# Memory queries in two token halves, rounding behind the second spatial mix, branch weights requested step by step

## The chip, the core and the metric

The kernel runs on one core of one Trainium2 chip. The metric is the device time of one execution in microseconds (us). The time before is the median of three runs, 2185.58 us (2185.37 to 2185.59). About 0.2% of it, 4.4 us, is what a measurement of this kernel can tell from no change.

## What is computed

One decoder layer over 1024 tokens of width 1024, all in float32: half a SwiGLU block, a mixing block with three branches, half a SwiGLU block. The change is in the mixing block:

```python
h = rmsnorm(x); z = h @ w_in
u, v = gelu(z[u]), gelu(z[v])
v = layernorm(v)                                   # chunks of 128 tokens, 8 groups of 64 channels
mixed = einsum('gts,bcsgd->bctgd', tril(w_s), v) + b_s
y_a = u * mixed                                    # branch a
y_b = mla(...)                                     # branch b, 8 heads, causal
q = rmsnorm(z[q_mem]); kv = rmsnorm(mem) @ w_kv    # 256 memory tokens, 4 heads of 128
k = rmsnorm(kv[:512]); s = q @ k.T * 128**-0.5
y_c = softmax(s) @ kv[512:]                        # branch c
merged = sum_i sigmoid(gate_i) * (y_i @ w_branch_i)
x = x + merged @ w_out
```

## The kernel before

Float32 products are made of three fast products. An operand is split in a rounded high part and a low part (`split`, L135: a cast on ScalarE, ACT, at L136, and a subtraction on VectorE, DVE, at L139), and `mm3` (L157) multiplies high by high (L160), high by low (L161) and low by high (L162). A weight can thus be used in full only when both engines have had their turn with it.

Tokens go in two halves of 512. The stretch in question is `sgu` (L570) and `mem_attention` (L824), about 1100 to 1205 us into the span. In program order it holds:

- `mem_kv` (L774) up to its first yield: the product for the memory keys, and their norm (`head_norm`).
- `split(1)` (L577), which rounds the second half of v, and a one-column Exp that brings in the table for the softmax (L610).
- `mix(0)` (L582): eight groups of three matmuls, each into a PSUM bank and from there to SBUF with a bias by ACT (L591), then for each of four channel blocks a load of u (L594), four transposes (L597), the product with u on DVE (L598), and `split_after` (L141; cast L142, subtraction L143).
- The rest of `mem_kv`: the product for the memory values, the keys turned and split into `kt` (L795, which ends in L152 on ACT and L153 on DVE), the values split into `vv` (L799).
- `mix(1)`: the same for the second token half.
- `mem_queries` (L814): the four heads' queries, high and low part, 8 loads of 128 x 1024 elements (512 KB), ordered behind the last load of u.
- `branches` (L503) of branch a, a generator. `weights` (L510) loads and splits 128 x 1024 weights for a pair of output blocks; a step loads the gate values (L521, 256 KB), does 12 matmuls of one block and one token half (`branch`, L551) and hands the bank to `sink_a` (L1044: L1045 on DVE, a store at L1046). The first three steps are blocks 0, 1, 2 of the first half, then the same of the second half, then each block's two halves. Blocks 0 and 1 use the first and the second 512 columns of the first pair of weights.
- `mem_attention`, which takes turns by a written list (L874): F is a branch step, S the scores of one tile of 128 tokens (12 matmuls of 256 columns, L834; then minimum L838, scaling L839, Exp L843, sum L847, scaling on GpSimd L848), T transposes, V the product with the values. It begins F, F, S, F, S, F, F, T, S.

PSUM gives this stretch four single banks ("bank", for the mix, the transposes and the branch steps) and two double ones ("mm", for the products of `mem_kv` and for the scores). In SBUF there are three raw buffers for unsplit weights, six rows "t" for u and the gates, and 16 "h" buffers.

The written order is not the order on the engines. In this stretch a planner of the framework orders them: when the program is built it runs a model of the machine (L2213), and gives an engine that is free the earliest instruction in program order whose inputs and buffers the model takes to be ready. On the chip each engine then keeps to its list. `after(i, first)` (L414) forces a place: i stands behind first on their common engine, without a semaphore. `self.hold` makes every cast of `split` stand behind an instruction in that way, and as long as it is set, `fetch` (L92) puts its load behind `self.queue`, the last store of the queries of branch b (L498). All DMAs here are issued by SyncE's queue (SP), in the planner's order.

Of the kernel before, what the change touches and what calls it, by code (L numbers as in the profile page):

```python
# [8 lines left out]
F32 = mybir.dt.float32  # L9
# [3 lines left out]
ACT = mybir.ActivationFunctionType  # L13
ALU = mybir.AluOpType
# [4 lines left out]
S = 1024  # L19
DT = D // P  # L20
NT = S // P
F = 2816
FT = F // P
SGW = 512
# [25 lines left out]
class Kernel:  # L50
# [1 line left out]


    def __init__(self, ctx, tc, a, out):
        self.tc, self.nc, self.a, self.out, self.last, self.hold = tc, tc.nc, a, out, None, None
        pool = lambda name, bufs=1, **k: ctx.enter_context(tc.tile_pool(name=name, bufs=bufs, **k))
        self.const = pool("const")
        self.small = pool("small", 4)
        self.hp = pool("hp", 16)
        self.xp = pool("xp", 10)  # L60
        self.wp = pool("wp")
        self.tp = pool("tp")
        self.ps = pool("ps", 1, space=bass.MemoryType.PSUM)
        self.dram = pool("dram", 1, space=bass.MemoryType.DRAM)
# [27 lines left out]
    def fetch(self, src, rooms=()):  # L92

        n, width = src.shape[1:]
        per, rooms = D // width, list(rooms)
        for k0 in range(0, n, per):
            m = min(per, n - k0)
            raw = rooms.pop(0)().rearrange("p a w -> p (a w)") if rooms else self.raw()
            raw = raw[:, :m * width]
            i = self.nc.sync.dma_start(raw, src[:, k0:k0 + m, :].rearrange("p k w -> p (k w)"))  # L100
            if self.hold is not None:
                self.after(i, self.queue)
            yield m, width, raw

# [30 lines left out]
    def split(self, hi, lo, src, eng=None):  # L135
        i = self.nc.scalar.copy(hi, src)  # L136
        if self.hold is not None:
            self.after(i, self.hold)
        return (eng or self.nc.vector).tensor_tensor(lo, src, hi.bitcast(F32), op=ALU.subtract)  # L139

    def split_after(self, hi, lo, src):  # L141
        i = self.nc.scalar.copy(hi, src)  # L142
        self.nc.vector.tensor_tensor(lo, src, hi.bitcast(F32), op=ALU.subtract)  # L143
        return i

    def split_later(self, hi, lo, src):

# [291 lines left out]
    def qkv(self, lat, asides):  # L439
# [3 lines left out]
        half = ROPE // 2  # L443
# [3 lines left out]
        T = 2  # L447
        with tc.tile_pool(name="qkvp", bufs=1) as p, tc.tile_pool(name="q1", bufs=1) as p1:
            for i0 in range(0, NT, 2):
# [45 lines left out]
                    nc.sync.dma_start(d, k[:, t].rearrange("p (g x) d -> p g (x d)", x=2))  # L495
                for t in range(T):
                    d = self.qd[:, :, i0 + t].rearrange("g p e -> p g e")
                    self.queue = nc.sync.dma_start(d, q[:, t].rearrange("p (g x) d -> p g (x d)", x=2))  # L498
                if i0 == T:
                    self.qk_mark = mark  # L500
                next(asides, None)
# [1 line left out]
    def branches(self, br, yt, sink):  # L503

        nc, a, w = self.nc, self.a, {}

        steps = [(dt, hf) for hf in range(2) for dt in range(3)]
        steps += [(dt, hf) for dt in range(3, DT) for hf in range(2)]

        def weights(d):  # L510
            if d not in w:
                x = self.load(a["w_branch"][br, d // 2])
                w[d // 2 * 2], w[d // 2 * 2 + 1] = x[:4], x[4:]

        weights(0)
        yield
        for n, (dt, hf) in enumerate(steps):
            for d, _ in steps[n:n + 2]:
                weights(d)
            sig = self.row()  # L520
            nc.sync.dma_start(sig, self.sig[br * DT + dt][:, hf])  # L521
            b = self.bank()
            self.branch(b, w[dt], yt, hf)
            sink(dt, hf, sig, b)
            yield
# [44 lines left out]
    def sgu(self, rows, p, sink):  # L570
        nc, a, tc = self.nc, self.a, self.tc
        v8 = lambda tag, hf, dt=F32R: (p if hf else self.pv).tile([P, 4, SGW], dt, name=tag)
        if True:
            w = self.parts_of(self.wss, P, self.split_pair)
            vs, yt = {}, []

            def split(hf):  # L577
                vs[hf] = v8("v_hi", hf), v8("v_lo", hf)
                for i, v in enumerate(rows[hf]):
                    self.v_mark = self.split(*(x[:, 2 * i:2 * i + 2] for x in vs[hf]), v)  # L580

            def mix(hf):  # L582
                if not yt:
                    yt.extend(self.split_pair() for _ in range(4))
                m, v = [self.h4().rearrange("p a w -> p (a w)") for _ in range(2)], vs[hf]
                views = [x.rearrange("p (c g d) -> p c g d", g=4, c=4) for x in m]
                for g in range(SGG):
                    b = self.bank()[:, :4 * SGW // SGG].rearrange("p (c d) -> p c d", c=4)
                    cols = slice(g * SGW // SGG, (g + 1) * SGW // SGG)
                    self.mm3(b, w[g], tuple(x[:, :, cols] for x in v), True, True)  # L590
                    nc.scalar.activation(views[g // 4][:, :, g % 4], b, ACT.Identity, bias=self.sg_b[:, g:g + 1])  # L591
                for j in range(4):
                    u = self.row()
                    z = nc.sync.dma_start(u, self.z[ZU + j][:, hf])  # L594
                    b = self.bank()
                    for c in range(4):
                        nc.tensor.transpose(b[:, c * P:(c + 1) * P], views[j // 2][:, c, 2 * j % 4:2 * j % 4 + 2], self.ident)  # L597
                    nc.vector.tensor_tensor(u, u, b, op=ALU.mult)  # L598
                    i = self.split_after(*(t[:, hf * 512:hf * 512 + 512] for t in yt[j]), u)
                return i, z  # L600

            self.hold = self.turned
            split(0)
            self.hold = None
            for v in rows[1]:
                self.layer_norm(v, self.qk_mark)
            kv = self.mem_kv(self.mem_t, self.mem_w)
            next(kv)
            split(1)
            nc.scalar.activation(self.stat("warm", 1), vs[1][0][:, 3, SGW - 1:].bitcast(F32), ACT.Exp, scale=0.0)  # L610
            mark, _ = mix(0)
            kv = next(kv)
            _, z = mix(1)
            rooms = [v8(n, 0).rearrange("p (a b) w -> p a (b w)", a=2) for n in ("v_hi", "v_lo")]
            late = self.mem_queries(1, iter([tuple(x[:, i] for x in rooms) for i in range(2)]), z)
            queries = self.mem_queries(0, iter(lambda: self.split_pair(self.h4), None), z) + late
            branch = self.branches(0, yt, sink)
            self.hold = mark
            next(branch)
            self.hold = None  # L620
            rooms = [v8(n, 1, F32) for n in ("v_hi", "v_lo")]
            rooms = [x.rearrange("p (a h) (b m) -> p a (h b) m", a=2, b=2)[:, k] for x in rooms for k in range(2)]
            return self.mem_attention(queries, rooms, *kv, branch)

    def head_norm(self, x, ps):

# [147 lines left out]
    def mem_kv(self, mt, w):  # L774
# [19 lines left out]
        for hh in range(0, MH, 2):  # L794
            self.to_feature(  # L795
                tuple(t[:, hh:hh + 2].rearrange("p h m -> p (h m)") for t in kt),
                [x[:, t, hh + k] for k in range(2) for t in range(2)], self.mk_g,
            )
        self.split(vv[0], vv[1], ps)  # L799
        yield kt, vv  # L800

# [9 lines left out]
            out += [tuple(t[:, i * 512:i * 512 + 512] for t in ts) for i in range(2)]  # L811
        return out

    def mem_queries(self, pair, rooms, first):  # L814

        out = []
        for o in range(2):
            qs = next(rooms)
            for t, src in zip(qs, self.mq[2 * pair + o]):
                self.after(self.nc.sync.dma_start(t.bitcast(F32), src), first)  # L820
            out.append(qs)
        return out

    def mem_attention(self, qt, rooms, kt, vv, filler):  # L824

        nc = self.nc
        r, nr = self.mq_r, self.mq_nr
# [2 lines left out]
        def scores(i, k):  # L830
            t = 2 * i + k
            sc = self.mm().rearrange("p a (b m) -> p (a b) m", b=2)
            for hh in range(MH):
                self.mm3(  # L834
                    sc[:, hh], tuple(x[:, t * P:(t + 1) * P] for x in qt[hh]), tuple(x[:, hh] for x in kt),
                    True, True)
            mx = self.stat("m_mx", MH)
            nc.vector.tensor_reduce(mx, sc, axis=AXX, op=ALU.min)  # L838
            nc.vector.tensor_tensor(mx, mx, r[:, t], op=ALU.mult)  # L839
# [30 lines left out]

        S, T, V = scores, turn, value
        F = lambda: next(filler, None)
        yt = [self.split_pair(self.h4) for _ in range(MH)]
        for f, *x in (  # L874
                (F,), (F,), (S, 0, 0), (F,), (S, 0, 1), (F,), (F,), (T, 0, 0), (S, 1, 0), (F,), (T, 0, 1), (S, 1, 1),
                (F,), (V, 0), (F,), (T, 1, 0), (S, 2, 0), (F,), (T, 1, 1), (S, 2, 1), (F,), (V, 1), (F,), (T, 2, 0),
                (S, 3, 0), (F,), (T, 2, 1), (S, 3, 1), (F,), (V, 2), (F,), (T, 3, 0), (F,), (T, 3, 1), (F,), (V, 3)):
            f(*x)
# [1338 lines left out]
```

## Time and profile before

| | |
|---|---|
| median of three runs | 2185.58 us |
| the profiled execution | 2181.75 us |
| its span | 2180.0 us |
| TensorE (PE) busy | 2160.0 us, 99% |
| DVE busy | 1574.5 us, 72% |
| ACT busy | 911.4 us, 42% |
| granted TensorE clock | 0.999 |

The profile is one execution. Its times count from the start of the span. Rows of the timeline give the start, the time from start to end, the engine, the line, the operation, what it writes and reads, and how many instructions are merged in the row; in brackets stands how long the engine was idle before, and who ended it. PE is TensorE's matmuls, SPq the issues of DMAs. Rows by windows give each engine's busy time in a stretch, with the granted clock, the busy share of the DMA engines and what they moved. An idle time counts for the whole only if it is on the engine that sets the end.

### The profile page before, as it was taken

The numbers are of one execution on the slowest core, as the hardware profiler recorded it, in microseconds if no ns is written. First come the engines' busy times: TensorE is split into PE (matmuls) and PEld (weight loads), VectorE is DVE, ScalarE is ACT, GpSimd is POOL, SyncE is SP. The second block draws the span as 40 slices with busy tenths as digits, with TensorE's granted clock in tenths as the row PEclk, the third lists the DMA queues.
The fourth block names the chain that finished last, engine by engine and source line by source line (L and its number), as shares of the span: only waits on it lengthen the run. The fifth ranks groups of instructions, "written<-read, shape, count | busy, mean of one in ns | idle before, by whom it ended". The sixth has DMA issues, their size and how long they took to land.

```text
span 2180.0 us, 27531 instructions
## 1 busy us (share of the span) xinstructions
PE 2160.0 (99%) x10154; PEld 1802.9 (83%) x10154; DVE 1574.5 (72%) x2374; ACT 911.4 (42%) x1491; POOL 273.5 (13%) x278
## 2 busy tenths in 40 slices
PE   9999999999999999999999999999999999999999
PEld 5888888888887888888988889988888888888887
DVE  7976666679889656655895679885886666657884
ACT  5433333343445334433554368833432222224332
POOL 2011111100000000000232321140011211210000
PEclk9999999999999999999999999999999999999999
DMA  4264554385433444541685731093043233337443
GB/s 146 92 218 163 185 176 174 137 319 172 130 116 104 147 166 166 209 147 61 231 320 217 266 121 59 30 351 123 34 140 102 93 101 99 114 130 291 169 130 106
DMA packets 128823, 340.98 MB, mean 156 GB/s; under 512 B 15152, under 2 KB 23472, under 8 KB 128688
## 3 DMA queue, kind: packets, MB, share of 16 engines
q1 hardware_dynamic: 128688, 339.22, 44.5%
q8 instruction: 80, 1.31, 0.2%
q14 instruction: 55, 0.45, 0.1%
HBM read 229.33 MB, written 109.84 MB: 156 GB/s over the span
## 4 chain that ended last, share of the span: by engine, by line
PE 91%; DVE 5%; ACT 2%; issue 1%; DMA 1%; POOL 0%; SPq 0%; ACTq 0%; DVEq 0%; POOLq 0%
PE one L160 15%; PE one L161 15%; PE one L162 15%; PE bank L160 12%; PE bank L162 12%; PE bank L161 12%; PE mm L160 2%; PE mm L161 2%; PE mm L162 2%; PE bank L968 1%; PE bank L983 1%; PE bank L984 1%; PE bank L432 1%; DVE wlo L149 1%; DVE wlo L139 0%
## 5 line engine op out<-in xcount | busy, mean ns | idle before, releaser
L148 ACT CAST whi<-x 128x1024 fp32r<-128x1024 f32 (+1 forms) x203 | 193.2, 955 | 419.4 <-PE one L161 141.7
L149 DVE TENSOR_TENSOR wlo<-x,whi 128x1024 fp32r<-128x1024 f32 (+1 forms) x203 | 242.2, 1194 | 57.9 <-ACT whi L148 21.6
L1376 DVE TENSOR_TENSOR t<-t,one 128x512 f32<-128x512 f32 x188 | 129.0, 686 | 194.0 <-PE one L162 193.8
L160 PE MATMUL bank<-h,whi 128*128 128x512 f32 x636 | 247.6, 390 | 0.0
L162 PE MATMUL bank<-h,wlo 128*128 128x512 f32 x636 | 247.5, 389 | 0.0
L161 PE MATMUL bank<-h,whi 128*128 128x512 f32 x636 | 247.5, 389 | 0.0
L160 PE MATMUL one<-h,whi 128*128 128x512 f32 x516 | 202.3, 392 | 0.0
L161 PE MATMUL one<-h,whi 128*128 128x512 f32 x516 | 201.5, 391 | 0.0
L162 PE MATMUL one<-h,wlo 128*128 128x512 f32 x516 | 201.3, 390 | 0.0
L160 PE MATMUL one<-w,whi 128*128 128x512 f32 x432 | 168.6, 390 | 0.0
L162 PE MATMUL one<-w,wlo 128*128 128x512 f32 x432 | 168.1, 389 | 0.0
L161 PE MATMUL one<-w,whi 128*128 128x512 f32 x432 | 168.1, 389 | 0.0
L139 DVE TENSOR_TENSOR wlo<-w,whi 128x1024 fp32r<-128x1024 f32 (+2 forms) x112 | 114.7, 1038 | 70.1 <-ACT whi L136 69.9
L136 ACT CAST whi<-w 128x1024 fp32r<-128x1024 f32 (+2 forms) x112 | 99.0, 901 | 149.8 <-PE bank L161 53.7
L1958 POOL TENSOR_TENSOR raw<-raw 128x512 f32<-128x512 f32 x38 | 56.9, 1498 | 783.6 <-DVE raw L1813 684.8
L162 PEld LDWEIGHTS bank<-h,wlo 128*128 128x128 f32 x636 | 119.4, 188 | 24.9
L161 PEld LDWEIGHTS bank<-h,whi 128*128 128x128 f32 x636 | 119.4, 188 | 24.7
L160 PEld LDWEIGHTS bank<-h,whi 128*128 128x128 f32 x636 | 119.4, 188 | 24.6
L160 PE MATMUL bank<-whi 128*128 128x512 f32 x352 | 136.9, 389 | 0.0
L161 PE MATMUL bank<-wlo,whi 128*128 128x512 f32 x352 | 136.9, 389 | 0.0
L162 PE MATMUL bank<-whi,wlo 128*128 128x512 f32 x352 | 136.9, 389 | 0.0
L162 PEld LDWEIGHTS one<-h,wlo 128*128 128x128 f32 x516 | 97.3, 189 | 20.3
(391 smaller groups left out, 4913.2 us busy)
## 6 DMA issues: line engine op xcount, KB each, us to landing
x<-in_ffn_w_gu_dram SPq DMA_DIRECT2D x78, 512.0 KB, 4.9
w<-tdt SPq DMA_DIRECT2D x40, 512.0 KB, 4.5
gate<-raw SPq DMA_DIRECT2D x33, 512.0 KB, 2.9
tdb<-raw SPq DMA_DIRECT2D x64, 256.0 KB, 2.2
h<-in_ffn_w_down_dram SPq DMA_DIRECT2D x64, 256.0 KB, 6.0
w<-tdb SPq DMA_DIRECT2D x30, 512.0 KB, 4.4
tdt<-w SPq DMA_DIRECT2D x48, 256.0 KB, 2.3
x<-in_w_gate_dram SPq DMA_DIRECT2D x22, 512.0 KB, 7.1
```

Source lines behind the costliest of these rows:

```text
L136: i = self.nc.scalar.copy(hi, src)
L139: return (eng or self.nc.vector).tensor_tensor(lo, src, hi.bitcast(F32), op=ALU.subtract)
L148: self.nc.scalar.copy(hi, src)
L149: return lambda: self.nc.vector.tensor_tensor(lo, src, hi.bitcast(F32), op=ALU.subtract)
L160: i = mmul(out, s[0], m[0], start=first, stop=False, **kw)
L161: mmul(out, s[0], m[1], start=False, stop=False, **kw)
L162: self.last = mmul(out, s[1], m[0], start=False, stop=last, **kw)
L432: nc.tensor.transpose(b[:m, k * P:(k + 1) * P], s, self.ident)
L968: nc.tensor.transpose(b[:, at:at + P], prs[t][:, kk * P:(kk + 1) * P], self.ident)
L983: nc.tensor.matmul(o, w, pt[0], start=n == 0, stop=False)
L1376: return self.nc.vector.tensor_tensor(out, x, y, op=ALU.add)
L1958: sub = lambda d, x, y: (eng or nc.gpsimd).tensor_tensor(d, x, y, op=ALU.subtract)
```

## The change

- `mix` takes a function `then`, called behind its eight groups. With it, `split(1)` and the Exp go from ahead of `mix(0)` to behind its last bias instruction (L591), and are held behind it. `mix` returns that L591 instruction, and u is split by `split`; `split_after` goes.
- `mem_kv` yields once more between the keys and the values. The split of the values, and the split of the first branch weights, are held on ACT behind the last L591 of `mix(1)` (called `after`); before, the weights were held behind the last cast of u in `mix(0)`, and the values not at all.
- Loads of branch a's weights stand on the SP queue behind the latest load of gate values (`sig_mark`), one pair at a time. Before, only the first had a place given.
- `mem_queries` loads one half of the tokens (8 loads of 256 KB) and is called twice from the list, behind the second and the third branch step's gate load. In those three steps (A) the splits of weights are held behind `after` too.
- The first score matmul of each of the first two score tiles stands on PE behind the last matmul of the branch step ahead of it in the list.

```diff
 fetch:
-            if self.hold is not None:
+            if self.queue is not None:
                 self.after(i, self.queue)
 branches:
         def weights(d):
             if d not in w:
+                self.queue = self.sig_mark
                 x = self.load(a["w_branch"][br, d // 2])
+                self.queue = None
...
-            nc.sync.dma_start(sig, self.sig[br * DT + dt][:, hf])
+            self.sig_mark = nc.sync.dma_start(sig, self.sig[br * DT + dt][:, hf])
 sgu:
-            def mix(hf):
+            def mix(hf, then=None):
...
-                    nc.scalar.activation(views[g // 4][:, :, g % 4], b, ACT.Identity, bias=self.sg_b[:, g:g + 1])
+                    i = nc.scalar.activation(views[g // 4][:, :, g % 4], b, ACT.Identity, bias=self.sg_b[:, g:g + 1])
+                if then:
+                    self.hold = i
+                    then()
+                    self.hold = None
...
-                    i = self.split_after(*(t[:, hf * 512:hf * 512 + 512] for t in yt[j]), u)
+                    self.split(*(t[:, hf * 512:hf * 512 + 512] for t in yt[j]), u)
...
-            split(1)
-            nc.scalar.activation(self.stat("warm", 1), vs[1][0][:, 3, SGW - 1:].bitcast(F32), ACT.Exp, scale=0.0)
-            mark, _ = mix(0)
+            def second():
+                split(1)
+                nc.scalar.activation(self.stat("warm", 1), vs[1][0][:, 3, SGW - 1:].bitcast(F32), ACT.Exp, scale=0.0)
+
+            mix(0, second)
+            next(kv)
+            after, z = mix(1)
+            rooms = [v8(n, 0).rearrange("p (a b) w -> p a (b w)", a=2) for n in ("v_hi", "v_lo")]
+            late = [tuple(x[:, i] for x in rooms) for i in range(2)]
+            queries = [self.split_pair(self.h4) for _ in range(2)] + late
+            branch = self.branches(0, yt, sink)
+            self.hold = after
+            next(branch)
             kv = next(kv)
-            _, z = mix(1)
...
-            self.hold = mark
-            next(branch)
-            self.hold = None
+            self.hold, self.sig_mark = None, z
 mem_kv:
+        yield
         self.split(vv[0], vv[1], ps)
 mem_queries:
+    def mem_queries(self, qs, half, first):
+        c = slice(half * 512, half * 512 + 512)
+        for ts, src in zip(qs, self.mq):
+            for t, x in zip(ts, src):
+                self.after(self.nc.sync.dma_start(t[:, c].bitcast(F32), x[:, c]), first)
 mem_attention:
+                last = self.last
-                self.mm3(
+                first = self.mm3(
...
+                if i == hh == 0:
+                    self.after(first, last)
...
+        Q = lambda half: self.mem_queries(qt, half, self.sig_mark)
+
+        def A():
+            self.hold = after
+            F()
+            self.hold = None
...
-                (F,), (F,), (S, 0, 0), (F,), (S, 0, 1), (F,), (F,), (T, 0, 0), (S, 1, 0), (F,), (T, 0, 1), (S, 1, 1),
+                (A,), (A,), (Q, 0), (S, 0, 0), (A,), (Q, 1), (S, 0, 1), (F,), (F,), (T, 0, 0), (S, 1, 0), (F,), (T, 0, 1), (S, 1, 1),
```

More of the change, by code (lines that the diff above doesn't have):

```diff
@@ L54, in __init__ @@
     def __init__(self, ctx, tc, a, out):
-        self.tc, self.nc, self.a, self.out, self.last, self.hold = tc, tc.nc, a, out, None, None
+        self.tc, self.nc, self.a, self.out, self.last, self.hold, self.queue = tc, tc.nc, a, out, None, None, None
         pool = lambda name, bufs=1, **k: ctx.enter_context(tc.tile_pool(name=name, bufs=bufs, **k))
@@ L139, in split @@
         return (eng or self.nc.vector).tensor_tensor(lo, src, hi.bitcast(F32), op=ALU.subtract)
[L141 to L144, printed above, removed]
     def split_later(self, hi, lo, src):
@@ L497, in qkv @@
                     d = self.qd[:, :, i0 + t].rearrange("g p e -> p g e")
-                    self.queue = nc.sync.dma_start(d, q[:, t].rearrange("p (g x) d -> p g (x d)", x=2))
+                    self.sig_mark = nc.sync.dma_start(d, q[:, t].rearrange("p (g x) d -> p g (x d)", x=2))
                 if i0 == T:
@@ L608, in sgu @@
             next(kv)
-            split(1)
-            nc.scalar.activation(self.stat("warm", 1), vs[1][0][:, 3, SGW - 1:].bitcast(F32), ACT.Exp, scale=0.0)
-            mark, _ = mix(0)
-            kv = next(kv)
-            _, z = mix(1)
[L614 to L617, printed above, removed]
-            self.hold = mark
-            next(branch)
-            self.hold = None
+            def second():
[10 more added lines that the diff above has]
+            next(branch)
+            kv = next(kv)
+            self.hold, self.sig_mark = None, z
             rooms = [v8(n, 1, F32) for n in ("v_hi", "v_lo")]
             rooms = [x.rearrange("p (a h) (b m) -> p a (h b) m", a=2, b=2)[:, k] for x in rooms for k in range(2)]
-            return self.mem_attention(queries, rooms, *kv, branch)
+            return self.mem_attention(queries, rooms, *kv, branch, after)
     def head_norm(self, x, ps):
@@ L812, in mem_weights, with mem_attention @@
         return out
[L814 to L824, printed above, removed]
+    def mem_queries(self, qs, half, first):
[3 more added lines that the diff above has]
+                self.after(self.nc.sync.dma_start(t[:, c].bitcast(F32), x[:, c]), first)
+    def mem_attention(self, qt, rooms, kt, vv, filler, after):
         nc = self.nc
```

## The prediction

> **What bounds the kernel now.** I read the page first, then busy time by windows, then the timelines of PE, ACT, DVE and SP where PE is not busy. The page:
>
> ```profile
> span 2180.0 us, 27531 instructions
> ...
> PE 2160.0 (99%) x10154; PEld 1802.9 (83%) x10154; DVE 1574.5 (72%) x2374; ACT 911.4 (42%) x1491; POOL 273.5 (13%) x278
> ...
> PE 91%; DVE 5%; ACT 2%; issue 1%; DMA 1%; POOL 0%; SPq 0%; ACTq 0%; DVEq 0%; POOLq 0%
> ```
>
> PE sets the end: it is idle for 20.0 us in all, and the chain that ended last is 91% PE. The change adds and removes no matmul, so it can only fill or open gaps on PE. The windows of the stretch that it touches (the first figure behind the length is PE's busy time, the last two are the DMA engines' share and GB/s):
>
> ```profile
> 1135.10:1137.90 2.80, 1.73 (x15) 1.52 (x13) 2.80 (x6) 2.55 (x5) 0.00 (x0) 1.00 1.01 407
> 1137.90:1144.20 6.30, 4.81 (x35) 4.18 (x35) 5.87 (x9) 5.88 (x14) 0.00 (x0) 1.00 1.01 395
> 1144.20:1154.00 9.80, 9.80 (x45) 8.09 (x44) 5.16 (x9) 2.04 (x4) 0.00 (x0) 1.00 1.03 408
> ...
> 1160.90:1168.10 7.20, 3.19 (x25) 2.93 (x25) 3.98 (x10) 4.48 (x16) 3.05 (x2) 1.00 0.66 226
> 1168.10:1260.00 91.90, 91.52 (x505) 79.26 (x504) 56.71 (x101) 38.58 (x108) 30.92 (x26) 1.00 0.63 233
> ```
>
> PE loses 1.07 + 1.49 us around the second mix and 4.01 us behind the first scores, 6.57 in all (0.30%). That is the ceiling of any gain from these gaps. Up to 1260 only 0.38 us more is lost, so what is won has nothing behind it in this block that must give it back.
>
> **The change part by part.** First the score gap, as it is the largest:
>
> ```profile
> 1154.00 0.28 PE L160 MATMUL mm<-h,h 128*128 128x256 f32 x1
> 1154.12 0.28 PE L161 MATMUL mm<-h,h 128*128 128x256 f32 x1
> ...
> 1160.56 0.40 PE L162 MATMUL bank<-x,wlo 128*128 128x512 f32 x1
> 1164.47 0.38 PE L160 MATMUL mm<-h,h 128*128 128x256 f32 x1 [3.52 <-ACT v_hi L843]
> ```
>
> ```profile
> 1158.99 2.35 DVE L838 TENSOR_REDUCE m_mx<-mm 128x4 f32<-128x1024 f32 x2 [8.40 <-PE mm L162]
> ```
>
> The first two score tiles start together at 1154.00 because their queries, 4 MB in whole rows, come late; they end together, and hold both double banks. The third tile is next on PE's list and waits until the first is through DVE and ACT, from DVE's minimum at 1158.99 to 1164.47, 5.5 us. After the change the first tile stands behind the second branch step and the second behind the third step, and two more steps come ahead of the third tile. A tile is 12 matmuls of 0.12 (1154.00 to 1154.12), 1.4 us. A step is 12 matmuls of twice the columns, 2.8; three steps and a tile, over 9 us, lie between the first tile's end and the third. The gap goes: **-4.0 us**, if the queries' first halves (2 MB) are there when PE comes to them; that is the third rival below.
>
> Now the second mix and the first branch step on PE, ACT and DVE.
>
> ```profile
> 1139.19 0.39 PE L160 MATMUL bank<-v_hi,x 128*128 128x256 f32 x1 [0.63 <-DVE h L153]
> ...
> 1144.13 0.48 PE L160 MATMUL bank<-x,whi 128*128 128x512 f32 x1
> 1144.44 0.40 PE L161 MATMUL bank<-x,whi 128*128 128x512 f32 x1
> 1144.68 0.40 PE L162 MATMUL bank<-x,wlo 128*128 128x512 f32 x1
> ```
>
> ```profile
> 1136.81 0.69 ACT L152 ACTIVATE h<-bank,c_mem_k_norm 128x512 fp32r<-128x512 f32 x1
> 1137.39 1.01 ACT L136 CAST h<-mm 128x1024 fp32r<-128x1024 f32 x1
> 1138.28 1.16 ACT L136 CAST whi<-raw 128x512 fp32r<-128x512 f32 x2
> 1139.32 1.22 ACT L591 ACTIVATE h<-bank,c_sg_b 128x256 f32<-128x256 f32 x3
> 1140.40 1.17 ACT L136 CAST whi<-raw 128x512 fp32r<-128x512 f32 x2
> 1141.43 1.97 ACT L591 ACTIVATE h<-bank,c_sg_b 128x256 f32<-128x256 f32 x5
> ```
>
> ```profile
> 1139.04 1.22 DVE L139 TENSOR_TENSOR h<-mm,h 128x1024 fp32r<-128x1024 f32 x1
> 1140.17 2.50 DVE L139 TENSOR_TENSOR wlo<-raw,whi 128x512 fp32r<-128x512 f32 x4
> 1143.10 2.48 DVE L598 TENSOR_TENSOR t<-t,bank 128x512 f32<-128x512 f32 x4 [0.43 <-PE bank L597]
> 1145.49 2.49 DVE L143 TENSOR_TENSOR x<-t,x 128x512 fp32r<-128x512 f32 x4
> ```
>
> The step's pace is 0.23 to 0.24 a matmul (1144.44 to 1144.68). The mix's bias instructions on ACT (L591), which free its banks, wait behind the cast of the values (1.01) and two of weights (1.16), and again behind two more (1.17). Held back, these leave ACT to eight L591 of about 0.40 (1.97 for five) from 1137.50, so the last could end at 1140.7 instead of 1143.40. The keys' turn on DVE (L153), which ended PE's wait at 1139.19, is not moved; if the fourth group still needs its bank, five more L591 follow at about 1139.8, and the last ends at 1141.8. I take 1141.2, **2.2 us earlier**, with 1.6 to 2.7 as its bounds. The transposes behind it then end at about 1141.9.
>
> But the first branch step needs the first half of its weights rounded on both engines, and that now starts at 1141.2 too. The third matmul of the step (1144.68) wants the low half, a DVE subtraction of 0.69 (2.50 for four). Before, these four ran in DVE's time while PE stood. Now they come due together with the eight operations on u (L598, L143), which stand earlier in program order. Nothing holds u behind the weights, the u rows keep DVE fed once they begin (in the trace all eight run without a gap between 1143.10 and 1147.98, 4.9 us), and the planner prefers what is earlier. So I take it that the weights' low half comes behind them: start at 0.3 before the last L591 as in the trace (1143.10 against 1143.40), 1140.9 + 4.9 + 0.7 = 1146.5, the third matmul at 1146.6. That is **1.9 us later** than 1144.68, against 2.2 earlier if it had been there in time; bounds by the same sum from 1140.7 and 1141.8 are 1.4 and 2.5. This step decides the size of the gain, and its order is what the trace of before cannot show.
>
> The other parts cost little. The held cast of the values (ACT 1.01, DVE 1.22) now stands behind the weights; its double bank is wanted by the second score tile at about 1154 (1146.6 + two steps and a tile), 7 us later, cover enough. The second pair of weights, on SP before at 1131.10 with two others, stands now behind the first gate load, and is wanted by the third step, at about 1153:
>
> ```profile
> 1131.10 1.43 SPq L100 DMA_DIRECT2D raw<-in_w_branch_dram  x3
> ...
> 1138.96 1.22 SPq L521 DMA_DIRECT2D t<-gate  x2
> 1140.48 4.86 SPq L820 DMA_DIRECT2D h<-mq  x4
> ```
>
> ```profile
> DMA to landing us min/median/max: 3.1/6.5/10.8
> ```
>
> (The last row is of L100, the weights' loads.) Requested at 1139.4 and with the median of 6.5 it is there at 1145.9, with the longest at 1150.2, and its split takes 2.4 us: in time either way, by 0.4 us at the worst. Without that cover each microsecond late is paid in full, since the second score tile stands behind that step. Eight more issues on SP at 0.4 us (1.43 for three with gaps) are 3 us of a queue that mostly waits; gate loads behind them are wanted a step at a time. The move of the split of v's second half behind the first mix changes nothing: its casts already run there, two of 1.0 us from 1129.32, behind the four L591 that end at 1128.95:
>
> ```profile
> 1127.38 1.57 ACT L591 ACTIVATE h<-bank,c_sg_b 128x256 f32<-128x256 f32 x4 [3.83 <-PE bank L162]
> 1129.32 2.00 ACT L136 CAST v_hi<-h 128x1024 fp32r<-128x1024 f32 x2 [0.37 <-DVE rs_b L180]
> ```
>
> Everything behind 1168 is planned anew as well; with PE idle 0.38 us in the next 92 I price that at nothing, and at 1 us to either side for the range.
>
> The sum: -4.0 + 1.9 = -2.1, and 0.1 for restarts saved (the first matmul of 256 columns after a wait takes 0.38 or 0.39, others 0.28): **-2.2 us**. The profiled execution, 2181.75 (span 2180.0 and 1.75 around it), would become 2179.6; the median stands 3.83 above it at 2185.58, and I take the same 2.2 off: **2183.4 us**. With the bounds above and the 1 us, this case runs from 2181.8 to 2185.0.
>
> **The rivals.**
>
> *The weights come through at once.* If the planner's model finds DVE free in the moment when the first cast is done, the low half is ready 0.6 + 0.7 after 1141.2, at 1142.5 to 1142.8 with an operation in hand ahead of it. PE then gains 1.9 here instead of losing 1.9: -5.9, 2179.7 us. For it speaks that DVE has nothing between the keys' turn (1139.04) and the first u; against it that u is ready at nearly the same moment and comes first in the order.
>
> *The gap moves on.* The scores are spread, but the planner's list is again wrong about something else (a gate row, the third tile) and PE loses about 2 us at another place: 2185.6, no difference. For it speaks that the present gap arose in just this way, a list made for queries that come early; against it that PE loses next to nothing from 1168 on with the same list.
>
> *The queries come too late, and now nothing may pass them.* Before, PE had branch steps to do until 1154.00. Now the first score tile stands behind the second step by force, in my sum at 1146.6 + 10 matmuls (2.3) + a step (2.7) = 1151.6, and the steps behind it wait with it. At the best eight loads of 256 KB follow the second gate load at the 400 GB/s of the windows: 5.2 us from about 1141.4, 1146.6. At the worst they find no free buffer earlier than the last of the four h loads did, which was issued at the end of its row, at 1145.0 (1140.48 + 4.86 - 0.3); for L820 the trace answers:
>
> ```profile
> DMA to landing us min/median/max: 6.7/9.0/10.4
> ```
>
> Then eight issues at 0.4 and the longest landing of 10.4 end at 1158.6, and PE waits 7.0 us: -2.2 + 7.0 = +4.8, 2190.4 us. It eats the gain from a landing at 1153.8 on. Against it speaks that 1 MB of weights now leaves the queue ahead of them, 2.6 us at 400 GB/s. [...]
>
> **How the numbers follow.** My case 0.42, weights at once 0.28, gap moved 0.18, queries late 0.12. Of 2183.4 the part below 2181.2 (faster by over 0.2%, 4.4 us, about what a measurement of this kernel can tell from no change) is about a sixth. Faster: 0.28 + 0.07 = 0.35. Slower by as much: 0.12 and 0.02 of the moved gap, 0.14. The same: 0.51. The range goes from 1 us below the first rival, 2178.8, to 2188.0, which leaves most of the late queries out.
>
> **What would show it.** Right: PE's wait for L843 gone; the last L591 of the second mix near 1141; one wait of PE at the first branch step for a DVE low half of about 4 us; the first two score tiles a branch step apart, with no wait for a DMA ahead of them. Wrong: that low half ahead of the u operations on DVE (then 2179.7), a PE wait for queries or weights (then above 2184), or a new gap for the third tile.

## The result, and the profile after

| | before | after |
|---|---|---|
| median, first comparison (7 executions of each) | 2185.37 us | 2177.42 us |
| lowest to highest | 2181.64 to 2185.94 | 2176.28 to 2178.74 |
| ratio, with its 95% interval | | 0.9968 (0.9957 to 0.998) |
| profiled execution | 2181.75 us | 2176.28 us |
| its span, PE busy, the rest | 2180.0, 2160.0, 20.0 | 2174.5, 2159.0, 15.5 |

The forecast was 2183.4 us with a range from 2178.8; the time lies below it. Between the two profiled executions 5.5 us are gone, 4.5 of them from PE's pauses (20.0 less 15.5). Between the medians it is 7.95 us, more than the 6.57 that the prediction called the ceiling.

The page of the kernel after:

```profile
span 2174.5 us, 27544 instructions
...
PE 2159.0 (99%) x10154; PEld 1802.9 (83%) x10154; DVE 1572.7 (72%) x2374; ACT 912.5 (42%) x1491; POOL 275.6 (13%) x278
```

Its windows of the touched stretch (length, then PE's busy time; PEclk is the third figure from the end):

```profile
1137.10:1142.20 5.10, 4.06 (x36) 3.99 (x35) 3.31 (x6) 4.81 (x13) 0.00 (x0) 1.00 0.91 271
1142.20:1150.70 8.50, 8.50 (x40) 6.93 (x38) 8.50 (x14) 4.18 (x8) 0.00 (x0) 1.00 1.05 364
1150.70:1161.10 10.40, 9.91 (x61) 8.55 (x59) 3.56 (x8) 4.49 (x16) 1.66 (x1) 1.00 0.97 329
1161.10:1168.10 7.00, 7.00 (x48) 6.49 (x49) 4.39 (x9) 4.42 (x13) 3.44 (x3) 1.00 0.78 292
```

Three losses of 1.07, 1.49 and 4.01 us have become two, 1.04 in the second mix and 0.49 in the scores. PE's timeline of after shows the branch's first matmuls and the score tiles:

```profile
1142.18 0.48 PE L155 MATMUL bank<-x,whi 128*128 128x512 f32 x1
1142.50 0.39 PE L156 MATMUL bank<-x,whi 128*128 128x512 f32 x1
...
1143.20 0.41 PE L157 MATMUL bank<-x,wlo 128*128 128x512 f32 x1
...
1150.71 0.28 PE L155 MATMUL mm<-h,h 128*128 128x256 f32 x1
...
1158.86 0.39 PE L155 MATMUL mm<-h,h 128*128 128x256 f32 x1
...
1161.05 0.39 PE L155 MATMUL mm<-h,h 128*128 128x256 f32 x1 [0.49 <-ACT v_hi L849]
```

The branch begins 1.95 us earlier than before (1144.13), and its third matmul, the first on a low half, at 1143.20, without a wait: until then PE had two matmuls of the next block. The first score tile starts at 1150.71 in place of 1154.00, and the third, at 1158.86, finds its bank free; only the fourth waits. ACT and DVE in that moment:

```profile
1138.81 2.40 ACT L588 ACTIVATE h<-bank,c_sg_b 128x256 f32<-128x256 f32 x6 [0.29 <-PE bank L157]
1141.09 1.15 ACT L136 CAST whi<-raw 128x512 fp32r<-128x512 f32 x2
1142.12 1.03 ACT L136 CAST h<-mm 128x1024 fp32r<-128x1024 f32 x1
1144.06 1.14 ACT L136 CAST whi<-raw 128x512 fp32r<-128x512 f32 x2 [0.91 <-DMA raw<-in_w_branch_dram]
1145.11 2.18 ACT L136 CAST x<-t 128x512 fp32r<-128x512 f32 x4
```

```profile
1141.15 1.28 DVE L599 TENSOR_TENSOR t<-t,bank 128x512 f32<-128x512 f32 x2 [1.79 <-PE bank L598]
1142.36 0.69 DVE L139 TENSOR_TENSOR wlo<-raw,whi 128x512 fp32r<-128x512 f32 x1
1142.96 0.68 DVE L599 TENSOR_TENSOR t<-t,bank 128x512 f32<-128x512 f32 x1
1143.56 0.69 DVE L139 TENSOR_TENSOR wlo<-raw,whi 128x512 fp32r<-128x512 f32 x1
...
1147.09 1.29 DVE L139 TENSOR_TENSOR x<-t,x 128x512 fp32r<-128x512 f32 x2
```

The planner set the weights' first low half behind two of the eight u operations, not behind all. The casts of u went to the end of ACT's list (1145.11), so u's subtractions came last on DVE.

### The profile page after: what moved, and what is told of

The parts are those of the page before. It is cut to its first block, busy times and chain, and to the rows that moved or that the text cites. A ratio compares the mean times of both kernels' runs of the same rounds, so it can differ in the third digit from the quotient of the medians.

```text
span 2174.5 us, 27544 instructions
## 1 busy us (share of the span) xinstructions
PE 2159.0 (99%) x10154; PEld 1802.9 (83%) x10154; DVE 1572.7 (72%) x2374; ACT 912.5 (42%) x1491; POOL 275.6 (13%) x278
## 4 chain that ended last, share of the span: by engine, by line
PE 89%; DVE 6%; ACT 2%; DMA 1%; issue 1%; POOL 1%; SPq 0%; ACTq 0%; DVEq 0%; POOLq 0%
PE one L155 15%; PE one L156 15%; PE one L157 15%; PE bank L155 12%; PE bank L156 12%; PE bank L157 12%; PE bank L981 1%; PE mm L155 1%; PE mm L157 1%; PE mm L156 1%; PE bank L996 1%; PE bank L997 1%; PE bank L427 1%; DVE wlo L144 1%; DMA t<-gate 0%
```

## The experiments

Theory: the weights' low half came through at once, and the pauses thus closed are the gain. The main rival formed on the way: the executions of one kernel differ among themselves because TensorE's granted clock differs, and that has to be taken apart from the pauses. Times are medians; "before" is the kernel before on the same chip, in 33 executions for the first four runs, 22 for the next four and 20 for the last three (2184.01, 2184.52, 2184.42). The runs of one such group share a chip. After was timed in the first comparison and again in the second group alone, so differences from it to the other runs are less exact than those from before.

**Before, once more.** No edit.

> The kernel before, unchanged, once more. Its seven executions so far are 2181.6, 2181.7, 2183.5 and four of 2185.4 to 2185.9; the one profiled was 2181.75, of the short kind. Theory A: the long executions lose some 4 us at one place on PE, in the touched stretch (the first score tiles, whose queries come late), so that the change removes it too; a profile of a long execution then shows PE's gap in front of the third score tile or ahead of the first one at 7 to 8 us in place of 4.0. Theory B: the 4 us lie elsewhere (the start, where PE stands for 11 us in all, or the end), and the median's 7.95 us is 5.5 of the change and 2.5 of how the executions fell. If the profile is of a short execution again, it tells nothing, and the spread alone is read: 2181.6 to 2185.9 in both theories.

2183.33 us in 11 executions, 2182.3 to 2185.89; ratio 1.0001 (0.9992 to 1.001). The profiled one was a long one, 2185.35:

```profile
span 2183.6 us, 27531 instructions
...
PE 2164.4 (99%) x10154; PEld 1807.5 (83%) x10154; DVE 1573.1 (72%) x2374; ACT 911.9 (42%) x1491; POOL 273.3 (13%) x278
```

The rest beside PE is 19.2 us, no more than the 20.0 of the short execution; the same 10154 matmuls took 4.4 us longer. The windows, of the long execution and then of the short one, show where (PEclk, the granted clock, is the third figure from the end):

```profile
40.00:44.00 4.00, 4.00 (x12) 3.23 (x12) 3.66 (x14) 1.04 (x1) 0.00 (x0) 0.50 0.00 0
44.00:48.00 4.00, 4.00 (x17) 3.20 (x16) 1.96 (x3) 0.34 (x1) 0.00 (x0) 0.76 0.00 0
...
1140.00:1150.00 10.00, 9.31 (x49) 8.17 (x50) 9.05 (x15) 7.83 (x17) 0.00 (x0) 0.83 0.99 382
...
1164.00:1168.00 4.00, 1.12 (x5) 1.13 (x6) 1.85 (x6) 3.47 (x13) 0.55 (x1) 0.69 0.62 207
1168.00:1172.00 4.00, 4.00 (x21) 4.00 (x21) 1.57 (x3) 1.66 (x7) 3.19 (x2) 0.50 0.90 288
```

```profile
40.00:44.00 4.00, 4.00 (x12) 3.09 (x11) 3.69 (x13) 1.05 (x1) 0.00 (x0) 0.60 0.00 0
44.00:48.00 4.00, 4.00 (x21) 3.34 (x20) 3.56 (x4) 2.08 (x3) 0.00 (x0) 1.00 0.00 0
...
1140.00:1150.00 10.00, 9.22 (x54) 8.00 (x55) 8.35 (x15) 5.81 (x13) 0.00 (x0) 1.00 1.02 402
...
1164.00:1168.00 4.00, 3.03 (x23) 2.83 (x24) 1.50 (x4) 2.61 (x10) 2.95 (x2) 1.00 0.84 281
1168.00:1172.00 4.00, 4.00 (x26) 3.49 (x24) 1.78 (x4) 3.09 (x10) 0.81 (x2) 1.00 0.73 267
```

The granted clock fell behind the pauses of the second mix (0.83 from 1140 to 1150) and behind the score gap (0.50 from 1168 to 1172), where the short execution kept 1.00, and it stayed down longer at 40 us (0.76 against 1.00 from 44 to 48), a place that the change does not touch. As busy time multiplied by the missing clock the mix has 9.31 x 0.17 = 1.6 us and the score gap 1.12 x 0.31 + 4.00 x 0.50 = 2.3 us, but that is not what they cost. For the cost one compares the start of the same matmul in both executions, since PE's list is the same. The product behind the start's half clock begins at 76.19 in place of 74.46: 1.7 us late. The second mix is reached 1.9 us late (1139.82 against 1137.93), the branch's first matmul only 2.4 us late (1146.54 against 1144.13), because the slow matmuls fill a pause of 0.78 us that PE otherwise has there. The third score tile is still 2.4 us late (1166.88 against 1164.47, behind the same pause of 3.52), the end 3.6. So about half of the difference comes from the start, as theory B held possible, and 1.7 us from the touched stretch, as theory A held, though in another form: no pause is longer, PE is slower behind it.

**The order that the prediction assumed.** In after:

```
+        j = (eng or self.nc.vector).tensor_tensor(lo, src, hi.bitcast(F32), op=ALU.subtract)
+        if self.low is not None:          # set for the first branch step only
+            self.after(j, self.low)       # = the last subtraction of u
```

> The kernel after, with the low half of the first branch weights forced behind the last subtraction of u on VectorE, the order that the prediction assumed. Theory (the failed step is this order alone): the third matmul of the first branch step comes at 1146.5 in place of 1143.2, so 3.3 to 3.4 us more than after: 2179.7 for a profiled execution, 2180.8 for the median. Rival: PE fills the wait with the high-half matmuls of the next blocks (four banks of two matmuls of 0.23), so that 1.4 us of it are hidden and the price is about 2 us. Second rival: the order costs nothing, since another bound stands right behind it (the queries or the second weights): 0 to 0.5 us.

2181.61 us (2179.95 to 2185.94), 2.4 below before; ratio to before 0.9992 (0.9983 to 1.0001), so by its interval anything from 3.7 us less to 0.2 more. DVE, PE:

```profile
1141.80 2.48 DVE L602 TENSOR_TENSOR t<-t,bank 128x512 f32<-128x512 f32 x4 [1.80 <-PE bank L601]
1144.20 1.22 DVE L139 TENSOR_TENSOR h<-mm,h 128x1024 fp32r<-128x1024 f32 x1
1145.37 2.50 DVE L139 TENSOR_TENSOR x<-t,x 128x512 fp32r<-128x512 f32 x4
1147.79 2.49 DVE L139 TENSOR_TENSOR wlo<-raw,whi 128x512 fp32r<-128x512 f32 x4
```

```profile
1148.53 0.79 PE L160 MATMUL bank<-x,wlo 128*128 128x512 f32 x1 [1.91 <-DVE wlo L139]
...
1149.55 0.63 PE L159 MATMUL bank<-x,whi 128*128 128x512 f32 x1
1149.97 0.63 PE L160 MATMUL bank<-x,wlo 128*128 128x512 f32 x1
```

The low half waits behind all of u, and its first matmul comes at 1148.53, not at 1146.5: the memory values' subtraction (1.22) now stands among the operations on u, and these begin 0.9 us later than the prediction's sum had them. PE's own loss there is 2.8 us in four pauses, since it took high-half matmuls first, as the rival said; but then it runs at 0.42 a matmul (1149.55 to 1149.97) in place of 0.23. Against after in its first comparison the order costs 3.7 us between the lowest executions (2179.95, 2176.28) and 4.2 between the medians. The theory's 3.4 is near, though by other parts; the rival's 2 us leaves out the slower clock.

**The two halves of the change alone.** First the second mix: queries as whole rows at the old place, later weights and score order as before.

> The second mix alone: casts of the memory values and of the branch weights held behind it as in the kernel after, but the queries in whole rows at their old place, no forced order of the score tiles, and the later weights' loads as before. Theory: the mix's 1.5 to 2.0 us are won (first branch matmul at 1142.2 in place of 1144.1) and the 4.0 us gap ahead of the third score tile stays: 2179.8 to 2180.3 for a profiled execution, 3.5 to 4.0 us above after. Theory A on the two lengths of before: this kernel has them too, some executions 4 us longer than the others. Rival: the earlier branch steps only reach the queries earlier, so that PE waits there for the same 2 us and nothing is won: 2181.8.

Then the scores: the cast of the values and those of the weights held no more behind the second mix, and the split of v's second half back ahead of the first.

> The scores alone: queries in halves, score tiles in the forced order and weights requested step by step as in the kernel after, but the casts of values and weights not held behind the second mix. Theory: the 4.0 us gap goes and the mix keeps its loss, so 2177.7 to 2178.2 for a profiled execution, 1.5 to 2.0 above after. Theory A: this kernel's executions lie within 2.5 us like those of after. Rival: without the held casts the weights' low half and u collide otherwise, and the whole is worth less than the parts: 2179 or more.

The mix alone: 2181.69 us, ratio 0.9989 (0.998 to 0.9998), the pause ahead of the third tile 4.09 us. The scores alone: 2180.05 us, 0.9984 (0.9975 to 0.9993). That is 2.3 and 4.0 us below before, each by its interval known to about 2 us; the sum, 6.3, agrees with what both together give below (6.8). The expected profiles, 2179.8 to 2180.3 and 2177.7 to 2178.2, were too low by 2.1 and 1.1. In the mix alone 1.8 us of that are the longer half clock at the start (granted 0.50 from 40 to 44 and 0.72 from 44 to 48, against 0.60 and 1.00; the product that begins at 74.46 in before begins at 76.26). In the scores alone a half clock in the stretch (0.42 to 0.43 us a matmul from 1146.42 to 1148.55) stands behind a pause of 2.28 us:

```profile
1144.45 1.74 PE L598 MATMUL bank<-ident,h 128*128 128x128 f32 x12 [2.28 <-ACT h L588]
```

```profile
1144.00:1148.00 4.00, 3.54 (x17) 3.16 (x18) 4.00 (x8) 3.55 (x8) 0.00 (x0) 0.71 1.05 402
```

The spreads don't fit theory A: the mix alone, with its long pause, spread over 1.9 us (2180.56 to 2182.45), the scores alone over 5.0.

**After, once more**, beside the next three.

> The kernel after, unchanged, beside the others on one chip. Theory C, formed from the repeated run of before (its profiled execution was 3.6 us longer than the first one and had granted clocks of 0.70 at 1140 and 0.50 at 1168, behind PE's pauses, where the first had 1.00): a pause of PE may be followed by some microseconds at half the clock, so that it is charged twice, and the change saves these as well as the pauses. Then after, which has no pause over 1.1 us in the touched stretch, has a narrow spread (2176 to 2179) and stands 5.5 us below before's fastest executions and 6.5 to 8 below its median. Rival: the slow clock comes and goes by itself, whatever PE does; then after spreads as widely as before (4.5 us) and the medians differ by 5.5.

2177.74 us in 5 executions (2176.41 to 2178.53), 6.8 below before; ratio 0.9966 (0.9953 to 0.9978). Its spread is 2.1 us, that of before 3.8 in this comparison. This fits theory C, and is no proof of it.

The granted clock over the span, on record for each execution, says more. In the 75 executions of before beside these runs it was 0.999 in 5, 0.998 in 24, 0.997 in 32 and 0.996 in 14; in the 12 of after it was 0.999 in 11 and 0.998 in one. Before's time goes with it: in its first 33 executions the medians are 2182.41, 2183.55, 2184.16 and 2186.04 us, from the highest clock to the lowest. At 0.999 before (2182.41) and after (2177.23, first comparison) lie 5.2 us apart, near to the 5.5 of the two profiles. So before runs with half clock more often than after, and this, not the pauses alone, is in the medians. That the pause brings the half clock is what the next two test.

**A pause where there was none.** In after, at one product of the second feed-forward part, n = 2 or 6:

```
+                for _ in range(n):
+                    nc.vector.scalar_tensor_tensor(
+                        hi, in0=a, scalar=0.0, in1=hi.bitcast(F32), op0=ALU.mult, op1=ALU.add)
```

> The kernel after, with a pause of PE put into the second feed-forward part, where PE never stands: the weights of one product are rewritten with themselves plus zero times the result of the product before, by two VectorE instructions of 0.7 us in a row, for which the next matmul waits. The output is the same. PE then stands for about 2 us. Theory C: the profile shows the granted clock at 0.5 for 3 to 7 us behind the pause in some executions, so that some are 2 us longer than after and others 4 to 5. Rival (the clock goes by itself): 2 us longer in all, the clock 1.00 behind the pause, with the spread of after.

> As the last, with six VectorE instructions in place of two: PE stands for about 4.5 us, as long as ahead of the third score tile in before. Theory C: half the clock behind it more often than behind the short pause, for 4 to 7 us: 6.5 to 8 us longer than after in most executions. Rival: 4.5 us longer in all, and the clock 1.00 behind it.

2182.25 and 2185.34 us: 4.5 and 7.6 above after. PE, with two instructions and with six:

```profile
1586.21 0.47 PE L155 MATMUL one<-w,whi 128*128 128x512 f32 x1 [3.02 <-DVE whi L1414]
...
1588.20 0.63 PE L156 MATMUL one<-w,whi 128*128 128x512 f32 x1
1588.63 0.63 PE L157 MATMUL one<-w,wlo 128*128 128x512 f32 x1
```

```profile
1591.21 0.76 PE L155 MATMUL one<-w,whi 128*128 128x512 f32 x1 [5.94 <-DVE whi L1414]
...
1592.20 0.63 PE L157 MATMUL one<-w,wlo 128*128 128x512 f32 x1
1592.63 0.63 PE L155 MATMUL one<-w,whi 128*128 128x512 f32 x1
```

The pauses are 3.0 and 5.9 us, longer than meant, and behind each the pace is 0.43 in place of 0.23. Each costs 1.5 to 1.8 us more than its length, in the medians and between the lowest executions (2181.02 and 2184.19 against 2176.41: 4.6 and 7.8). The granted clock over the span was 0.998 or less in all 20 executions, where it was 0.999 in all five of after. So the pause brings the half clock with it; that it goes by itself is refuted for this place.

**The parts of the score half.** The queries as whole rows, all at the place of the first halves:

```
+        if half == 0:
-                self.after(self.nc.sync.dma_start(t[:, c].bitcast(F32), x[:, c]), first)
+                    self.after(self.nc.sync.dma_start(t.bitcast(F32), x), first)
```

> The kernel after with the queries loaded in whole rows again, all eight loads (4 MB) at the place of the first halves; all else as after. It tells whether the halves matter. Theory: 4 MB at 400 GB/s take 10.4 us from 1139.1 to 1145 on, so the first score tile can't start at 1150.7 but only at 1154 or later, as in before; PE fills that with branch steps until their weights run out, and the gap ahead of the third tile comes back in part: 2 to 4 us above after (2178.5 to 2180.5 for a short execution), and with a pause of that length a spread as wide as before's. Rival: the earlier place is what counts, the halves don't: within 0.5 us of after.

And the later weights no more held behind the gate loads (`self.queue = self.sig_mark if d == 0 else None`):

> The kernel after without the third part of the change: the first pair of the branch's weights is asked for where it was, but the later pairs are no longer held behind the gate loads, so that 1 MB of weights leaves ahead of the queries again, as in before. Theory: the queries' first halves land 2.6 us later (1 MB at 400 GB/s), the first score tile starts some 2.5 us later, and up to 2.5 us come back as a pause: 0.5 to 2.5 us above after. Rival: the queries wait for their rooms, not for the channel, and nothing changes.

2181.54 us, ratio to before 0.9991 (0.9982 to 1.0), and 2178.33 us, 0.9974 (0.9964 to 0.9984): 3.8 and 0.6 above the repeat of after, which ran on another chip. PE of the one, then of the other (first and third score tile):

```profile
1157.40 0.28 PE L155 MATMUL mm<-h,h 128*128 128x256 f32 x1
...
1165.57 0.51 PE L155 MATMUL mm<-h,h 128*128 128x256 f32 x1 [4.69 <-ACT v_hi L849]
```

```profile
1152.66 0.28 PE L155 MATMUL mm<-h,h 128*128 128x256 f32 x1
...
1161.04 0.39 PE L155 MATMUL mm<-h,h 128*128 128x256 f32 x1 [1.45 <-ACT v_hi L849]
```

Without the halves the whole score gap is back. The steps of the weights are worth 0.6 us between the medians, the low end of what was expected, and with intervals that overlap this is not clear of noise; the profile does show the first score tile 1.95 us later than in after and a pause of 1.45 us ahead of the third. The third piece, the forced order of the tiles, was not run: without it the built program is the same, instruction by instruction, so it decides nothing here.

**Two tries at a better version.** In the first the keys' transposes stand ahead of the last quarter of the values' product. An order on PE forces this.

> The kernel after, with the transposes of the memory keys moved ahead of the last quarter of the values' product, so that the keys' turn on ScalarE and VectorE comes earlier and the pause of 1.04 us in the second mix goes. Theory: 0.6 to 1.0 us less than after (2175.3 for a short execution), and with theory C no half clock at all in this stretch. Rival: the weights' low half now comes behind three u products in place of two and the third matmul waits for it: no gain, or 0.5 us lost.

In the second the first norm's column sums stand four products later, and the next weights are rounded ahead of them.

> The kernel after with one more edit elsewhere, where its longest pause is: at 36 to 39 us PE waits 2.9 us for GpSimd's additions ahead of the column sums of a norm, and matmuls run at half clock from 40 to 43 or 47 in every profile so far. The column sums are put behind four more products and the rounding of the next weights ahead of them. Theory C: the pause of 2.9 us shrinks to under 1.5, and the half clock behind it, 1.6 to 3.4 us more, goes with it or shrinks: 2 to 5 us less than after, 2172.5 to 2175.5. Rival: another wait (for the weights' low half or for the norm's scale) takes its place at once and the clock falls all the same: within 1 us of after.

2177.87 us, ratio 0.9966 (0.9954 to 0.9978), and 2178.16 us, 0.9973 (0.9962 to 0.9983): neither beats after. In the first the pause of 1.04 is gone, but the keys' transposes now wait 1.20 us for a bank that u's products hold. The second is the more telling. PE of after, then of this kernel:

```profile
39.22 1.05 PE L389 MATMUL bank<-ones,t 128*128 128x1 f32 x8 [2.87 <-POOL t L1234]
...
74.98 0.47 PE L155 MATMUL one<-x,whi 128*128 128x512 f32 x1 [0.53 <-DVE raw L1389]
```

```profile
51.03 0.50 PE L157 MATMUL one<-h,wlo 128*128 128x512 f32 x1 [0.63 <-DVE wlo L144]
57.18 0.50 PE L155 MATMUL one<-h,whi 128*128 128x512 f32 x1 [0.85 <-ACT t L1502]
69.00 0.47 PE L155 MATMUL bank<-w,whi 128*128 128x512 f32 x1 [0.64 <-DVE t L1389]
76.06 0.47 PE L155 MATMUL one<-x,whi 128*128 128x512 f32 x1 [1.26 <-DVE raw L1389]
```

The pause of 2.87 is gone, the clock never falls (granted 1.00 from 40 to 48, against 0.57 from 40 to 44 in after), and yet PE reaches the same product 1.1 us later. It gave everything back in four waits for DVE and ACT. In after's profiled execution their chain thus sets the end of this stretch, and PE's pause and its half clock of 3.4 us only filled the time. That has a limit: where the half clock there lasts twice as long, as in the long execution of before (6.8 us by its granted clocks of 0.89, 0.50 and 0.76 in the three windows from 36 to 48), PE falls 1.7 us behind.

## Why the prediction was wrong, step by step

- **Score gap, -4.0.** Right in its mechanism: the pause of 3.52 is gone, 0.49 is left at the fourth tile, 3.5 in all. The first two tiles are not a whole branch step apart, as was said, but interleaved with branch matmuls; it is the earlier start (1150.71) and the steps behind it that free the bank. The later the first tile, the longer the wait ahead of the third: none in after, 1.45 us with a start at 1152.66, 4.69 with one at 1157.40.
- **Second mix, 2.2 us earlier.** Right: the last bias instruction ends at 1141.21 (1138.81 + 2.40), where 1141.2 was said.
- **The failed step:** "So I take it that the weights' low half comes behind them" (the eight operations on u). It came behind two. The third matmul ran at 1143.20, not at 1146.6: a gain in place of the +1.9 loss. Its ground, "the planner prefers what is earlier", could not carry it: the planner takes the earliest instruction that its model holds ready, and the sum had no account of what is ready when. DVE's list in after has the low half ahead of the third product with u, and the subtractions of u last, behind casts that ACT began only at 1145.11. When its model held each ready is not recorded. With the order forced, the median was 2.4 us below before, where 2.2 was forecast, but this closeness is in part luck: the low half was used at 1148.53 and not at 1146.6, PE hid a part of the wait behind other matmuls, and the half clock, which is in no term of the sum, made up for it. What happened is the rival "weights come through at once": 5.9 us by its sum, 5.5 between the profiles.
- **Second weights, values, queries.** All in time for PE, as said. ACT waited 0.91 us for the second weights, and no PE wait came of it. The rival of the late queries did not come; the whole rows show that its danger lay in the bytes: with 4 MB asked for at that place the gap stays (4.69 us).
- **The ceiling of 6.57 us** was wrong in principle. It counted PE's pauses and took PE's busy time as fixed. The medians fell by 7.95 and, in the repeat, 6.8 us; the profiles by 5.5 and the lowest executions by 5.3 (2181.58 to 2176.28). The rest, 1.5 to 2.5 us, is by this reading half clock behind before's pauses: the long execution, with half clock there, was 1.7 us longer in the touched stretch than the short one without, and the clocks of all executions say that before mostly runs below the clock of its profiled execution. They don't say in which stretch an execution lost it, so the split between the medians stays inferred.
- **The step from the profiled execution to the median** (3.83 us, carried over unchanged) failed for the same cause: in after it is 1.1 (2177.42 less 2176.28). Of the 6.0 us between forecast and result 3.3 lie between the profiled executions (5.5 us gained in place of 2.2), mostly the failed step, and 2.7 in this one.
- **A slip in the working.** A sixth of the main case was counted as faster, below 2181.2, though its own bounds begin at 2181.8. It doesn't change the outcome.

## What to carry to other kernels

Where a planner orders the work, an order that decides the sign of a term is a case with its own chance, not an assumption: neither program order nor who is fed first foretells it. A pause of PE can be charged twice, by its length and by the half clock behind it: those of 3.0 and 5.9 us put in here cost 4.5 and 7.6 us. So closing one can bring more than its length, provided that PE, and not the chain beside it, sets the end of the stretch. Read the spread of the executions, and the clock of each, ahead of the sum: a kernel whose profile is one of its lowest executions hides a cost that the profile doesn't show. And place a difference between two executions by the start of the same instruction in both, not by busy time and clock: half of the long execution's excess arose 1100 us ahead of the stretch in question.

## What the runs showed of the hardware

Behind a pause the pace of a 512-column matmul went from 0.23 to 0.43 us (with two instructions put in, 1586.51 to 1586.74 and then 1588.20 to 1588.63). By the granted clocks of the windows the half clock lasts 3.4 or 6.8 us in these profiles: 3.4 with two instructions put in (0.94 and 0.63 in the windows of 4 us from 1584), 6.8 at the score gap in the long execution of before (0.69, 0.50 and 0.96 in those from 1164).

Pauses of 2.28, 2.87, 3.02, 4.09, 4.69 and 5.94 us were followed by it (granted 0.71, 0.57, 0.63, 0.73, 0.71 and 0.50 in a window of 4 us there), and so were two of 1.09 and 0.63 us in that long execution (0.70 from 1140 to 1144); in after a pause of 1.04 was not (1.00 from 1136 to 1148), nor were two of 1.08 and 0.64 in the scores alone (1.00 from 1136 to 1144), and the pause of 3.52 us in before once was (0.50 from 1168 to 1172) and once was not (1.00).

So in these runs the length of a pause alone does not tell whether the clock falls behind it; they do not show what does.
